# Sample outer products over 128 rows, with the keys held twice, in a hybrid recurrent decoder step

## The chip, the cores and the metric

The kernel runs on one core of one Trainium2 chip. The metric is the device time of one execution in microseconds (us). TensorE (PE) multiplies matrices and writes to PSUM; loading its weights is listed apart as PEld. VectorE (DVE), ScalarE (ACT) and GpSimd (POOL) work element by element, and SyncE (SP) only issues transfers. Each engine works through its own queue in order. Transfers are issued here from the queues of SP and POOL, a few from ACT's.

## The reference, cut to what matters

One inference step of one decoder layer, for a prompt of 256 tokens and for 8 sample sequences of 4 tokens each. Everything is float32. The three branches (an RG-LRU, a gated linear attention or GLA, and an mLSTM) read one projection, their outputs are merged with gates, and a squared-ReLU MLP follows. GLA and mLSTM carry a matrix state for every head and sequence, four heads each:

```python
# GLA, per chunk: state S (128 x 256 per head)
o = einsum('bhid,bhde->bhie', qe, S) + einsum('bhij,bhje->bhie', A, v_)
S = exp(bL[..., 0, :])[..., None] * S + einsum('bhjd,bhje->bhde', k_ * exp(bL - b), v_)
# mLSTM, per chunk: state C (256 x 256 per head), normaliser n
num = ci[..., None] * einsum('bhid,bhde->bhie', q_, C) + einsum('bhij,bhje->bhie', S, v_)
C = cs[..., None, None] * C + einsum('bhj,bhjd,bhje->bhde', wj, k_, v_)
n = cs[..., None] * n + einsum('bhj,bhjd->bhd', wj, k_)
```

For a sample sequence a chunk is its 4 tokens, so a new state is the old one, scaled, plus an outer product of keys and values over 4 tokens. All 8 sequences' states are read, used, updated and written back: 8 tiles of 128x1024 for GLA, and 16 tiles of 128x1028 for mLSTM (a column of each state holds the normaliser).

## The kernel before, in words

**The weight stream.** All large products go through `stream`: tiles of 128x1024 weights are loaded by SP, split by ACT (L156, a rounded part `hi`) and DVE (L157, the rest `lo`) and multiplied in three matmuls per block, L171 to L173, each 128x128 by 128x288 into PSUM tiles named mm. Raw, hi and lo have three buffers each. One step of the stream is one weight tile: 24 matmuls.

**The side work.** The branches' own work is written as generators, `gla()` and `mlstm()`, put beside the stream with `beside`. After each step of the stream, `run` advances each of them by one `yield`. What it issues there has high priority, but is put behind the step's last matmul and its hi and lo. A planner, which works from its own costs, then fixes the order on each engine except SP, whose order is the program's. `issue_after(x)` adds that an instruction may not come before x on the same engine. Of later use are `do(s, f, ...)`, which enters f in the list of step s, and `steps`, which issues one list per yield, in the order of entry. In `mlstm`, `when(n)` is the step of sample tile n, 5 + 3n/2 rounded down, so two tiles take three steps. GLA's tile n has step 3 + 2n.

**The samples.** `parts` writes keys and values, rounded to fp32r, in 128 rows: rows 0 to 63 are for one half of the sequences and rows 64 to 127 for the other, with 16 rows for a sequence, which hold high and low parts of its four tokens. The rows are repeated for all four heads along the free dimension: `kp` holds the keys, `vp` the values. `spread` (L668) makes from one head's values four copies `vx[:, b]`, in each of which only the rows of one sequence of each half are kept. A half call of it writes two of the four copies.

**A tile.** `tile_(n)` of either branch

- multiplies the queries with the old state (L870 or L1254; four products 128x32, side by side in the array, each in two instructions), with the tokens' own part added for the first tile of a head (L872, L1257);
- forms four outer products (L876, L1262), each over the 64 rows of one half, `kp[r, h, ...]` by `vxs[h][r, ...]`, 256 columns wide, into two PSUM buffers `pu` from `misc()` (tiles px, two buffers, shared with all other side work);
- lets DVE scale the old state and add the product (L879, L1267), in mLSTM also the normaliser's column (L1269);
- issues the tile's store from POOL (L880, L1270).

**Loads.** `load(n)` (L856, L1239) issues the load of tile n from POOL. Four buffers take turns: two of tag `st` and two inside a slot. A load of tile n has to wait until the store of tile n-4 has landed. In mLSTM, it is entered four steps ahead of its tile. POOL's queue also carries element-wise work, such as the sums of the merge at L961.

**Values.** In both branches `vx2` holds the spread values of two heads in turn. In mLSTM the two halves for head h are entered two and five steps behind the first tile of head h-1.

Of the kernel before, what the change touches and what calls it, by code (L numbers as in the profile page):

```python
# [8 lines left out]
F32 = mybir.dt.float32  # L9
F32R = mybir.dt.float32r  # L10
AF = mybir.ActivationFunctionType
ALU = mybir.AluOpType
AX = mybir.AxisListType

P = 128
# [38 lines left out]
def trunk(ctx, tc, io):  # L54
    nc = tc.nc
    PSUM = bass.MemoryType.PSUM
    V, S, G, T, Q = nc.vector, nc.scalar, nc.gpsimd, nc.tensor, nc.sync
# [19 lines left out]
    def slot(i, dt=F32):  # L77
        return big.tile([P, 8, N], dt, tag=f"s{i}", name=nm(f"s{i}"))

    def flat(t):  # L80
        return t.rearrange("p a n -> p (a n)")

    def misc():
        return px.tile([P, 512], F32, tag="px", name=nm("px"))
# [12 lines left out]
    def C(n):  # L97
        a, w = COFF[n]
        return con[:, a:a + w]
# [327 lines left out]
    for k in range(KT):  # L427
# [5 lines left out]
        r = slice(32 * (k % 4), 32 * (k % 4) + 32)  # L433
        T.matmul(ps[r, :N], ones[:, 0:32], sq, start=k < 4, stop=k >= KT - 4, skip_group_check=True)
    t = t288()
# [4 lines left out]
    for k, n in ((0, 2), (2, 2), (4, 4), (8, 4), (12, 4)):  # L440
        t = (xa, xb)[k // 8][:, k % 8:k % 8 + n, :]
# [35 lines left out]
    for i, p in enumerate((". L L L LV .", "L LL LL LV LLV .", "L L . L LV . L L . LLV . .", "L L . L LV . L L . LLV . .", "L L L L . V . L L . V .")):  # L477
        k0, k1, _ = STAGES[i]
# [156 lines left out]
    def copies(t):  # L635

        src = ident.rearrange("p (h x g t) -> p h g x t", h=4, x=4, g=2)
        for h in range(4):
            for g in range(2):
                a = P * h + 64 * g  # L640
                G.tensor_copy(t[:, a:a + 64].rearrange("p (x r t) -> p x r t", x=4, r=4), src[:, h, g].unsqueeze(2).to_broadcast([P, 4, 4, 4]))
        return t.rearrange("p (h i) -> p h i", h=4)
# [7 lines left out]
    def parts(dst, src, rep, lo):  # L650

        n, w = dst.shape[1:]
        p = misc()[:, 0:n * w].rearrange("p (h e) -> p h e", h=n)
        for h in range(n):
            T.matmul(p[:, h], rep[:, h], src, start=True, stop=True)
        S.copy(dst, p)
        for h in range(0, n, 256 // w):
            r = slice(h, h + 256 // w)
            t = t288()[:, 0:256].rearrange("p (h e) -> p h e", e=w)
            S.activation(t, p[:, r], AF.Copy, scale=lo[:, 0:1])  # L660
            V.scalar_tensor_tensor(dst[:, r], dst[:, r].bitcast(F32), lo[:, 1:2], t, ALU.mult, ALU.add)

    K_LO, V_LO = C("klo"), C("vlo")

    def spread(vx, v, half):

        for b in range(2 * half, 2 * half + 2):
            S.activation(vx[:, b], v.bitcast(F32), AF.Copy, scale=C("seq")[:, b:b + 1])  # L668
# [31 lines left out]
    def gla():  # L700
# [8 lines left out]
        for h in range(4):  # L709
            p = misc()  # L710
# [23 lines left out]
        dec = sc([P, 4, 12], "dec", 1)  # L734
# [13 lines left out]
        for t in range(2):  # L748
            for q in range(2):
                p = misc()  # L750
# [5 lines left out]
        p = misc()  # L756
# [5 lines left out]
        p = misc()  # L762
# [21 lines left out]
        for t in range(2):  # L784
            p = misc()
# [5 lines left out]
            if t == 0:  # L791
                by_sequence(qm, smp(qe))
                asb = sc([P, NS], "asb", 1)
                p = misc()
# [9 lines left out]
        for h in range(5):  # L804
            if h < 4:
                st = sp.tile([P, 1028], F32, tag="st", name=nm("st"), bufs=2)[:, 0:1024].rearrange("p (c e) -> p c e", c=4)
                pu = misc(), misc()
# [9 lines left out]
            if h:  # L817
                i = h - 1
                po = longp()
                for e in range(2):  # L820
                    for t in range(2):
                        c0 = e * 256 + t * P
                        T.matmul(po[:, c0:c0 + P], vt[:, t, i * 256 + e * P:i * 256 + (e + 1) * P], am[:, t, i, :],
                                 start=e == 0 and t == 0, stop=False, skip_group_check=True)
                for c in range(1, 4):
                    for e in range(2):
                        c0 = e * 256 + c * 64
                        T.matmul(po[:, c0:c0 + 64], sts[i][:, c - 1, e * P:(e + 1) * P], qe[:, i, c * 64:c * 64 + 64],
                                 start=False, stop=True, skip_group_check=True)
# [3 lines left out]
        kv = flat(slot(3, F32R))  # L833
        kp = kv[:, 0:512].rearrange("p (h d) -> p h d", h=4)
        vp = kv[:, 512:1536].rearrange("p (h e) -> p h e", h=4)
        rep = copies(bb[:, 0:512])
        yield
        sums = bb[:, 0:N]
        vx2 = flat(slot(4, F32R))[:, 0:2048].rearrange("p (i b e) -> p i b e", i=2, b=4)
# [4 lines left out]
        tiles, vxs, pos = {}, {}, {}  # L844
# [4 lines left out]

        def second():  # L850
            parts(vp[:, 2:4], vs[:, 0:256], rep[:, 2:4], V_LO)

        def load(n):
            i = n % 4
# [7 lines left out]
        def tile_(n):  # L862
            h, q = n // 2, n % 2
            if q == 0:
                pos[h] = longp()
            po = pos[h]
            s4 = tiles[n][:, 0:1024].rearrange("p (b e) -> p b e", b=4)
            for j in range(4):
                b = 4 * q + j
                T.matmul(po[32 * j:32 * j + 32, 0:256], qm[:, h, NS * b:NS * b + NS], s4[:, j, :], start=q == 0, stop=q == 1, skip_group_check=True)  # L870
            if q == 0:
                T.matmul(po[0:32, 0:256], asb[:, h], vs[:, 0:256], start=False, stop=False, skip_group_check=True)  # L872
            pu = [misc().rearrange("p (i e) -> p i e", i=2) for _ in range(2)]
            for j in range(4):
                b, r = 4 * q + j, slice(64 * (j % 2), 64 * (j % 2) + 64)
                T.matmul(pu[j % 2][:, j // 2], kp[r, h, :], vxs[h][r, b // 2, :], start=True, stop=True)  # L876
            for j in range(4):
                b, s = 4 * q + j, s4[:, j, :]
                V.scalar_tensor_tensor(s, s, dec[:, h, 4 + b:5 + b], pu[j % 2][:, j // 2], ALU.mult, ALU.add)  # L879
            G.dma_start(io["o_gla_s"][n], tiles[n][:, 0:1024])  # L880
            if q == 1:
                pos[h] = sc([P, 257], "os", 1)
                S.copy(pos[h][:, 0:256], po[:, 0:256])
# [175 lines left out]
    def mlstm():  # L1059
# [21 lines left out]
        for h in range(2):  # L1081
            r = slice(4 * h, 4 * h + 4)
# [6 lines left out]
        mr, xr, srow, scol, csb, col = (gates_[n] for n in ("mr", "xr", "srow", "scol", "csb", "col"))  # L1089
# [4 lines left out]
        for t in range(2):  # L1094
            for q in range(2):
                p = misc()
                for i in range(4):
                    n = 4 * q + i
# [5 lines left out]
        p = misc()  # L1104
        for h in range(4):
            for e in range(2):
                n = 2 * h + e
# [3 lines left out]
        p = misc()  # L1111
        for h in range(4):
            for e in range(2):
                n = 2 * h + e
# [3 lines left out]
        for t in range(2):  # L1118
            for q in range(2):
                p = misc()  # L1120
                for i in range(4):
                    n = 4 * q + i
                    T.matmul(p[:, i * P:(i + 1) * P], mc[:, n, t * P:(t + 1) * P], bdk[:, n * P:(n + 1) * P], start=True, stop=True)
                for i in range(2):
                    h = 2 * q + i
# [7 lines left out]
        for n in range(8):  # L1133
            p = misc()
# [6 lines left out]
        p = misc()  # L1141
# [3 lines left out]
        p = misc()  # L1145
# [9 lines left out]
        p = misc()  # L1155
        for h in range(4):
            for e in range(2):
                n = 2 * h + e
# [7 lines left out]
        for h in range(4):  # L1166
            p = misc()
# [6 lines left out]
            p = misc()  # L1174
            for e in range(2):
                n = 2 * h + e
                T.matmul(p[:, 0:256], mc[:, n, 0:P], tf[:, n, 0:NP], start=e == 0, stop=e == 1)
            for e in range(2):
                n = 2 * h + e
# [39 lines left out]
        mn = sc([P, 2], "gn5", 1)  # L1219
        V.tensor_scalar(mn, Pm("mn"), 0.5, None, ALU.mult)  # L1220
        sums = row("rr")
        tiles, vxs, pos, sqs = {}, {}, {}, []
        vx2 = flat(slot(2, F32R))[:, 0:2048].rearrange("p (i b e) -> p i b e", i=2, b=4)
        yield

        def part(dst, src, i, los):
# [9 lines left out]
        def load(n):  # L1236
            i = n % 4
            tiles[n] = sp.tile([P, 1028], F32, tag="st", name=nm("st"), bufs=2) if i < 2 else s9[:, 1028 * (i - 2):1028 * (i - 1)]
            G.dma_start(tiles[n], io["mC"][n])  # L1239

        def values(h, half):
            vxs[h] = vx2[:, h % 2]
            spread(vxs[h], vp[:, h], half)

        def tile_(n):
            h, q = n // 4, n % 4
            if q == 0:
                pos[h] = longp()
            po = pos[h]
            s4 = tiles[n].rearrange("p (b d e) -> p b d e", b=2, d=2)  # L1250
            for i in range(2):
                for d in range(2):
                    b, j = 2 * q + i, 2 * i + d
                    T.matmul(po[32 * j:32 * j + 32, 0:257], qm[:, 2 * h + d, NS * b:NS * b + NS], s4[:, i, d, :],  # L1254
                             start=q == 0, stop=q == 3, skip_group_check=True)
            if q == 0:
                T.matmul(po[0:32, 0:257], psb[:, h], vs, start=False, stop=False, skip_group_check=True)  # L1257
            pu = [misc().rearrange("p (d e) -> p d e", d=2) for _ in range(2)]
            for d in range(2):
                for i in range(2):  # L1260
                    r = slice(64 * i, 64 * i + 64)
                    T.matmul(pu[i][:, d], kp[r, h, d * P:(d + 1) * P], vxs[h][r, q, :], start=True, stop=True)  # L1262
            for i in range(2):
                b = 2 * q + i
                for d in range(2):
                    s = s4[:, i, d, 0:256]
                    V.scalar_tensor_tensor(s, s, csb[:, h, b:b + 1], pu[i][:, d], ALU.mult, ALU.add)  # L1267
                s = s4[:, i, :, 256]
                V.scalar_tensor_tensor(s, s, csb[:, h, b:b + 1], pnb[:, h, :, b], ALU.mult, ALU.add)  # L1269
            G.dma_start(io["o_C_s"][n], tiles[n])  # L1270
            if q == 3:
                pos[h] = sc([P, 257], "os", 1)
                S.copy(pos[h], po[:, 0:257])
# [21 lines left out]
        def do(s, f, *a):  # L1295
            at.setdefault(s, []).append(lambda: f(*a))

        def when(n):
            return 5 + n * 3 // 2
# [3 lines left out]
        do(1, part, kp, ks, 1, K_LO)  # L1303
        do(1, part, vp, vs[:, 0:256], 1, V_LO)
        do(2, ends)
        do(2, values, 0, 0)
        do(3, values, 0, 1)
        for n in range(16):
            do(when(n), tile_, n)
            do(when(n) - 4, load, n)  # L1310
        for h in range(1, 4):
            do(when(4 * h - 4) + 2, values, h, 0)
            do(when(4 * h - 4) + 5, values, h, 1)
        for h in range(4):
            e = when(4 * h + 3)
            do(e + 1, gather, h)
# [148 lines left out]
    h = ff1(0)  # L1465
# [144 lines left out]
```

## Time and profile before

| | us |
|---|---|
| median of 3 runs | 1980.32 |
| lowest and highest | 1979.65, 1981.12 |
| profiled execution | 1977.5 |
| its span, first to last instruction | 1975.7 |
| granted TensorE clock, mean | 0.993 of full |

| engine | busy us | share of the span |
|---|---|---|
| PE | 1940.9 | 98% |
| PEld | 1835.9 | 93% |
| DVE | 1045.2 | 53% |
| ACT | 801.1 | 41% |
| POOL | 233.4 | 12% |

GLA's sample tiles run from about 450 to 512 us of the span, those of mLSTM from about 725 to 832. How to read the rows further down: times are us from the start of the span. A row of the timeline has start, length, engine, line, operation, the tile written `<-` the tiles read, rows*columns of the weights, the moving operand, and how many instructions (`x4`) were merged; in brackets stands the engine's idle time before it and what ended it. A matmul is in flight longer than the distance to the next one, since the array is pipelined: cost is read from start to start. A row of the waits has who waited for whom, us in total, times, the longest. A row of the groups has busy us and the mean ns of one, then the idle time before.

### The profile page before, as it was taken

The page shows a single profiled execution, that of the slowest core. Times are in us where ns is not written, and L with a number is a line of the kernel's source. Part 1 is how long each engine was busy: PE and PEld are TensorE (multiplying, and loading weights), DVE is VectorE, ACT ScalarE, POOL GpSimd, SP SyncE. Part 2 cuts the span into 40 slices and gives each one's busy share as a digit, 9 for nine tenths or more (in the row PEclk, how much of TensorE's full clock was granted, in tenths as well). Part 3 has the DMA queues.
Part 4 walks back from the last instruction along what each step waited for, and adds up shares of the span by engine and source line. Part 5 has one row for each costly group of instructions (what it writes and reads, how often), then busy time and mean ns, then how long its engine had stood idle before and what let it go on. Part 6 is the DMA issues. An engine that isn't in the chain of part 4 may idle for free.

```text
span 1975.7 us, 35634 instructions
## 1 busy us (share of the span) xinstructions
PE 1940.9 (98%) x14944; PEld 1835.9 (93%) x14944; DVE 1045.2 (53%) x1580; ACT 801.1 (41%) x1106; POOL 233.4 (12%) x333
## 2 busy tenths in 40 slices
PE   6999999999999999999999999999999999999997
PEld 5899989998999998899999999999999999999997
DVE  5665737535673456554444564444444445454565
ACT  4233474534454343343333354443333334343433
POOL 0000200011042111101013331000000000010101
PEclk8999999999999999999999999999999999999999
DMA  9887757547443358856778645444444444444443
GB/s 379 341 307 287 289 200 271 203 154 282 163 154 126 129 192 267 311 195 273 278 296 344 239 152 186 156 172 164 163 171 160 160 168 173 166 163 164 161 162 121
DMA packets 109568, 416.99 MB, mean 211 GB/s; under 512 B 11568, under 2 KB 11744, under 8 KB 105696
## 3 DMA queue, kind: packets, MB, share of 16 engines
q1 hardware_dynamic: 100368, 382.34, 52.0%
q0 software_dynamic: 8032, 28.99, 4.3%
q10 hardware_dynamic: 1008, 3.39, 0.5%
q8 instruction: 117, 1.92, 0.4%
q14 instruction: 43, 0.35, 0.0%
HBM read 397.86 MB, written 16.81 MB: 210 GB/s over the span
## 4 chain that ended last, share of the span: by engine, by line
PE 94%; DMA 4%; DVE 1%; issue 0%; ACT 0%; SPq 0%; POOL 0%; DVEq 0%; ACTq 0%; POOLq 0%
PE mm L171 28%; PE mm L173 28%; PE mm L172 28%; PE pa L275 4%; DMA raw<-win 2%; DMA o_C_s<-st 1%; PE px L573 0%; DMA o_C_s<-s 0%; PE px L1262 0%; DVE lo L157 0%; PE px L810 0%; DMA st<-mC 0%; PE px L1189 0%; PE px L128 0%; PE pi L1254 0%
## 5 line engine op out<-in xcount | busy, mean ns | idle before, releaser
L157 DVE TENSOR_TENSOR lo<-raw,hi 128x1024 fp32r<-128x1024 f32 x450 | 556.3, 1238 | 556.0 <-ACT hi L156 536.2
L156 ACT ACTIVATE hi<-raw 128x1024 fp32r<-128x1024 f32 x450 | 476.5, 1060 | 842.0 <-PE mm L172 638.5
L171 PE MATMUL mm<-xh,hi 128*128 128x288 f32 x2576 | 763.4, 300 | 6.3 <-ACT xh L420 5.7
L172 PE MATMUL mm<-xl,hi 128*128 128x288 f32 x2576 | 760.2, 297 | 0.3 <-DVE xl L421 0.3
L173 PE MATMUL mm<-xh,lo 128*128 128x288 f32 x2576 | 744.6, 296 | 0.7 <-DVE lo L157 0.6
L171 PEld LDWEIGHTS mm<-xh,hi 128*128 128x128 f32 x2576 | 482.6, 188 | 27.1 <-issue 9.0
L171 PE MATMUL mm<-s,hi 128*128 128x288 f32 x1664 | 491.4, 298 | 0.3 <-ACT s L942 0.2
L172 PEld LDWEIGHTS mm<-xl,hi 128*128 128x128 f32 x2576 | 485.8, 189 | 3.9 <-issue 1.7
L172 PE MATMUL mm<-s,hi 128*128 128x288 f32 x1664 | 488.2, 295 | 0.0
L173 PEld LDWEIGHTS mm<-xh,lo 128*128 128x128 f32 x2576 | 480.8, 189 | 2.8 <-DVE lo L157 1.2
L173 PE MATMUL mm<-s,lo 128*128 128x288 f32 x1664 | 476.8, 295 | 0.4 <-DVE lo L157 0.4
L171 PEld LDWEIGHTS mm<-s,hi 128*128 128x128 f32 x1664 | 311.8, 188 | 6.6 <-issue 3.7
L172 PEld LDWEIGHTS mm<-s,hi 128*128 128x128 f32 x1664 | 312.5, 188 | 0.3
L173 PEld LDWEIGHTS mm<-s,lo 128*128 128x128 f32 x1664 | 308.3, 188 | 1.1 <-DVE lo L157 0.7
L157 DVE TENSOR_TENSOR lo<-s,hi 128x1024 fp32r<-128x1024 f32 x80 | 98.0, 1225 | 113.8 <-ACT hi L156 113.8
L156 ACT ACTIVATE hi<-s 128x1024 fp32r<-128x1024 f32 x80 | 84.9, 1061 | 140.8 <-PE mm L172 140.1
L1439 POOL TENSOR_TENSOR t<-t 128x288 f32<-128x288 f32 x64 | 60.2, 952 | 639.2 <-ACT t L1438 639.2
L472 DVE TENSOR_TENSOR s<-s,mm 128x288 f32<-128x288 f32 x96 | 41.9, 451 | 42.6 <-PE mm L173 41.7
L275 PE MATMUL pa<-s,silc 128*32 128x128 f32 (+2 forms) x720 | 53.1, 411 | 5.5 <-DMA s<-wad 5.5
L1455 DVE TENSOR_TENSOR s<-s,mm 128x288 f32<-128x288 f32 x96 | 40.3, 450 | 33.9 <-PE mm L173 32.6
L961 POOL TENSOR_TENSOR s<-s,t 128x288 f32<-128x288 f32 x32 | 31.7, 1020 | 190.8 <-DVE t L960 190.8
L275 PEld LDWEIGHTS pa<-s,silc 128*32 128x32 f32 x720 | 21.8, 112 | 23.1 <-issue 10.4
(383 smaller groups left out, 1096.3 us busy)
## 6 DMA issues: line engine op xcount, KB each, us to landing
raw<-win SPq DMA_DIRECT2D x192, 512.0 KB, 4.5
raw<-wf SPq DMA_DIRECT2D x176, 512.0 KB, 4.1
s<-wf SPq DMA_DIRECT2D x80, 512.0 KB, 3.2
s<-wada SPq DMA_DIRECT2D x26, 1024.0 KB, 8.7
s<-wad SPq DMA_DIRECT2D x24, 1024.0 KB, 9.1
ag<-wada SPq DMA_DIRECT2D x22, 1024.0 KB, 5.5
raw<-wout SPq DMA_DIRECT2D x32, 512.0 KB, 5.5
st<-wada SPq DMA_DIRECT2D x20, 512.0 KB, 7.3
```

Of the source, the lines that this page charges most:

```text
L156: pace["hi"] = S.activation(hi, raw, AF.Copy)
L157: pace["lo"] = V.tensor_tensor(out=lo, in0=raw, in1=hi.bitcast(F32), op=ALU.subtract)
L171: T.matmul(pss[m][:, :N], hi[:, kk, ms], xh, start=k == k0, stop=False)
L172: T.matmul(pss[m][:, :N], hi[:, kk, ms], xl, start=False, stop=False)
L173: pace["last"] = T.matmul(pss[m][:, :N], lo[:, kk, ms], xh, start=False, stop=k == kt - 1)
L275: pace["prod"] = T.matmul(ps[32 * j:32 * j + 32, h * w // 4:(h + 1) * w // 4], silu_c(k), v[:, j], start=k == 0 and h == 0, stop=k == KT - ...
L472: V.tensor_tensor(out=dst[:, base + m, :], in0=dst[:, base + m, :], in1=p, op=ALU.add)
L961: G.tensor_tensor(out=a, in0=a, in1=t, op=ALU.add)
L1439: G.tensor_tensor(out=r, in0=r, in1=r, op=ALU.mult)
L1455: V.tensor_tensor(out=a, in0=a, in1=p, op=ALU.add)
```

## The change

- A new helper, `by_half`, makes two copies of the keys on ACT, each scaled with a column of the constant `half`, 1 in the rows of one half and 0 in the others: `kps[0]` is kp itself, with the lower 64 rows kept, `kps[1]` the other.
- The outer products now run over all 128 rows, `kps[i]` by all rows of `vxs[h]`; the zeroed rows leave the other half's part out. The two products of one `pu` buffer stand together, followed by the DVE updates that read them, and then the second buffer's.
- In mLSTM the second keys take the place of one of the two heads' values, so one head's values are held at a time. Their spreads are entered one step behind tiles 4h-2 and 4h-1.
- In mLSTM, load n (from 4 on) is entered one step behind tile n-3 and issued after the store of tile n-3. The first four are as before.

```diff
+    def by_half(kp, other):
+
+        for i, t in ((1, other), (0, kp)):
+            S.activation(t, kp.bitcast(F32), AF.Copy, scale=C("half")[:, i:i + 1])
+        return kp, other
...
 (gla)
+        kps = kp, kv[:, 1536:2048].rearrange("p (h d) -> p h d", h=4)
...
         def second():
             parts(vp[:, 2:4], vs[:, 0:256], rep[:, 2:4], V_LO)
+            by_half(*kps)
...
-            pu = [misc().rearrange("p (i e) -> p i e", i=2) for _ in range(2)]
-            for j in range(4):
-                b, r = 4 * q + j, slice(64 * (j % 2), 64 * (j % 2) + 64)
-                T.matmul(pu[j % 2][:, j // 2], kp[r, h, :], vxs[h][r, b // 2, :], start=True, stop=True)
-            for j in range(4):
-                b, s = 4 * q + j, s4[:, j, :]
-                V.scalar_tensor_tensor(s, s, dec[:, h, 4 + b:5 + b], pu[j % 2][:, j // 2], ALU.mult, ALU.add)
+            for i in range(2):
+                pu = misc().rearrange("p (j e) -> p j e", j=2)
+                for j in range(2):
+                    T.matmul(pu[:, j], kps[j][:, h, :], vxs[h][:, 2 * q + i, :], start=True, stop=True)
+                for j in range(2):
+                    b = 4 * q + 2 * i + j
+                    s = s4[:, 2 * i + j, :]
+                    V.scalar_tensor_tensor(s, s, dec[:, h, 4 + b:5 + b], pu[:, j], ALU.mult, ALU.add)
...
 (mlstm)
-        vx2 = flat(slot(2, F32R))[:, 0:2048].rearrange("p (i b e) -> p i b e", i=2, b=4)
+        v2 = flat(slot(2, F32R))
+        vx = v2[:, 0:1024].rearrange("p (b e) -> p b e", b=4)
+        kps = kp, v2[:, 1024:2048].rearrange("p (h d) -> p h d", h=4)
...
-            G.dma_start(tiles[n], io["mC"][n])
+            with tc.issue_after(stores[n - 3].ins) if n >= 4 else nullcontext():
+                G.dma_start(tiles[n], io["mC"][n])
...
-            vxs[h] = vx2[:, h % 2]
-            spread(vxs[h], vp[:, h], half)
+            vxs[h] = vx
+            spread(vx, vp[:, h], half)
...
-            pu = [misc().rearrange("p (d e) -> p d e", d=2) for _ in range(2)]
-            for d in range(2):
-                for i in range(2):
-                    r = slice(64 * i, 64 * i + 64)
-                    T.matmul(pu[i][:, d], kp[r, h, d * P:(d + 1) * P], vxs[h][r, q, :], start=True, stop=True)
             for i in range(2):
                 b = 2 * q + i
+                pu = misc().rearrange("p (d e) -> p d e", d=2)
+                for d in range(2):
+                    T.matmul(pu[:, d], kps[i][:, h, d * P:(d + 1) * P], vxs[h][:, q, :], start=True, stop=True)
                 for d in range(2):
                     s = s4[:, i, d, 0:256]
-                    V.scalar_tensor_tensor(s, s, csb[:, h, b:b + 1], pu[i][:, d], ALU.mult, ALU.add)
+                    V.scalar_tensor_tensor(s, s, csb[:, h, b:b + 1], pu[:, d], ALU.mult, ALU.add)
...
-            G.dma_start(io["o_C_s"][n], tiles[n])
+            stores.append(G.dma_start(io["o_C_s"][n], tiles[n]))
...
+        do(2, by_half, *kps)
         do(2, values, 0, 0)
...
-            do(when(n) - 4, load, n)
+            do(when(n) - 4 if n < 4 else when(n - 3) + 1, load, n)
         for h in range(1, 4):
-            do(when(4 * h - 4) + 2, values, h, 0)
-            do(when(4 * h - 4) + 5, values, h, 1)
+            do(when(4 * h - 2) + 1, values, h, 0)
+            do(when(4 * h - 1) + 1, values, h, 1)
```

More of the change, by code (lines that the diff above doesn't have):

```diff
@@ L1221, in mlstm @@
         sums = row("rr")
-        tiles, vxs, pos, sqs = {}, {}, {}, []
-        vx2 = flat(slot(2, F32R))[:, 0:2048].rearrange("p (i b e) -> p i b e", i=2, b=4)
+        tiles, vxs, pos, sqs, stores = {}, {}, {}, [], []
+        v2 = flat(slot(2, F32R))
+        vx = v2[:, 0:1024].rearrange("p (b e) -> p b e", b=4)
+        kps = kp, v2[:, 1024:2048].rearrange("p (h d) -> p h d", h=4)
         yield
```

## The prediction

> **What bounds the kernel now.** I read the page first: which engine is full, and what the chain of work that ended last is made of.
>
> ```profile
> PE 1940.9 (98%) x14944; PEld 1835.9 (93%) x14944; DVE 1045.2 (53%) x1580; ACT 801.1 (41%) x1106; POOL 233.4 (12%) x333
> PE 94%; DMA 4%; DVE 1%; issue 0%; ACT 0%; SPq 0%; POOL 0%; DVEq 0%; ACTq 0%; POOLq 0%
> ```
>
> TensorE sets the time: a microsecond taken from its queue is a microsecond of the total, and work elsewhere costs nothing until TensorE waits for it. The second view is busy time by stretch, over the two places that the change touches: the sample tiles of GLA, then those of mLSTM.
>
> ```profile
> 450.00:512.00 62.00, 62.00 (x484) 53.85 (x482) 35.42 (x60) 24.04 (x36) 6.78 (x13) 1.00 0.67 243
> 720.00:835.00 115.00, 112.45 (x841) 94.75 (x841) 70.10 (x148) 37.96 (x53) 22.16 (x36) 1.00 0.82 279
> ```
>
> The columns are length, then busy time and count of PE, PEld, DVE, ACT and POOL, granted clock, DMA share, GB/s. GLA's stretch has no idle PE; mLSTM's has 2.55 us, at full clock. But "busy" hides gaps between pipelined matmuls, so the third view is PE's timeline, read by start times: what does a group of side matmuls add between two matmuls of the weight stream? The groups of matmuls by shape give the changed lines; the timeline shows them in place.
>
> ```profile
> L1262 PE MATMUL px<-s,s 64*128 64x256 f32 x64 | 13.0, 329 | 0.0
> L876 PE MATMUL px<-s,s 64*128 64x256 f32 x32 | 5.0, 329 | 0.0
> ...
> 645.25 0.30 PE L173 MATMUL mm<-xh,lo 128*128 128x288 f32 x1
> 645.38 1.03 PE L1189 MATMUL px<-s,s 128*128 128x257 f32 x4
> ...
> 646.38 0.29 PE L172 MATMUL mm<-s,hi 128*128 128x288 f32 x1
> ...
> 726.22 0.50 PE L1262 MATMUL px<-s,s 64*128 64x256 f32 x4
> ...
> 727.03 0.29 PE L173 MATMUL mm<-xh,lo 128*128 128x288 f32 x1
> ...
> 728.63 0.29 PE L173 MATMUL mm<-xh,lo 128*128 128x288 f32 x1
> 728.85 0.64 PE L1254 MATMUL pi<-st,s 128*32 128x257 f32 x8
> ...
> 729.66 0.30 PE L172 MATMUL mm<-xl,hi 128*128 128x288 f32 x1
> ...
> 731.26 0.29 PE L172 MATMUL mm<-xl,hi 128*128 128x288 f32 x1
> 731.48 0.50 PE L1262 MATMUL px<-s,s 64*128 64x256 f32 x2
> 731.91 0.40 PE L173 MATMUL mm<-xh,lo 128*128 128x288 f32 x1
> 732.15 0.29 PE L171 MATMUL mm<-xh,hi 128*128 128x288 f32 x1
> ...
> 737.02 0.29 PE L173 MATMUL mm<-xh,lo 128*128 128x288 f32 x1
> 737.25 0.64 PE L1254 MATMUL pi<-s,s 128*32 128x257 f32 x8
> 737.82 0.50 PE L1262 MATMUL px<-s,s 64*128 64x256 f32 x4
> ...
> 738.48 0.30 PE L172 MATMUL mm<-xl,hi 128*128 128x288 f32 x1
> ...
> 741.41 0.29 PE L173 MATMUL mm<-xh,lo 128*128 128x288 f32 x1
> ...
> 742.20 0.50 PE L1262 MATMUL px<-s,s 64*128 64x256 f32 x2
> ...
> 742.87 0.29 PE L172 MATMUL mm<-xl,hi 128*128 128x288 f32 x1
> ...
> 829.77 0.50 PE L1262 MATMUL px<-s,s 64*128 64x256 f32 x2
> ```
>
> The stream steps every 0.133 us (727.03 to 728.63 is twelve steps). From 731.26 to 732.15 lie 0.89 us where two steps would take 0.27: one lone pair of half-row products costs 0.62 us. The tile's read products alone (L1254, 128*32) cost 728.63 to 729.66, 0.77 more than two steps. With four half-row products behind them the added time is 1.19 (737.02 to 738.48), with two it is 1.19 as well (741.41 to 742.87): attached to L1254 a group of either size costs 0.43. In the group of four, products of the upper and the lower half run side by side, so they cost no more than two of one half. A lone group of another data type but full 128*128 shape (645.25 to 646.38, four in 0.86, 0.216 each) is far longer in matmul work, yet it fits 257 columns at a constant rate and leaves no room for a fixed part. So I take the half-row pair's cost to be mostly the change of shape, paid on the way in and out.
>
> Counted through that timeline from the first group (726.22) to the last (829.77), mLSTM's 64 products are 15 lone pairs, 5 attached pairs and 6 attached fours; GLA's 32 are 2 lone pairs, 2 attached pairs and 6 attached fours. **Old price:** 17 x 0.62 + 19 x 0.43 = 10.5 + 8.2 = 18.7 us.
>
> **The products over 128 rows.** The same 96 matmuls, each now 128*128 with the other half's rows zeroed in the keys. No row shows this shape with 256 columns in one pass, so I bound it.
>
> ```profile
> 748.98 0.29 PE L171 MATMUL mm<-xh,hi 128*128 128x288 f32 x1
> 749.11 0.30 PE L1280 MATMUL px<-rd,ones 128*128 128x32 f32 x2
> ...
> 749.47 0.30 PE L173 MATMUL mm<-xh,lo 128*128 128x288 f32 x1
> ```
>
> Two tiny 32-column products add 0.22, so 0.11 each is the lower end; the stream's 288-column step of the same data type, 0.133, is the upper end. I take it by columns from the latter, which is nearest: 256/288 x 0.133 = 0.1185. New price 96 x 0.1185 = 11.4 (10.6 to 12.8), **a gain of 7.3 us (5.9 to 8.1)**. By group: a lone pair falls from 0.62 to 0.24, an attached pair from 0.43 to 0.24, an attached four rises from 0.43 to 0.47, since its halves no longer overlap. L1254 keeps its own 0.77. How the planner splits the groups no longer matters, which makes this term robust against another order.
>
> [...]
>
> **Loads behind the next store.** POOL's timeline holds the mC loads (L1239) and the stores (L1270), in one queue in order; PE's timeline shows who waits.
>
> ```profile
> 757.74 0.53 POOL L1239 DMA_DIRECT2D s<-mC  x1 [7.34 <-DMA o_C_s<-s]
> 758.27 0.54 POOL L1270 DMA_DIRECT2D o_C_s<-st  x1
> 766.73 0.53 POOL L1239 DMA_DIRECT2D st<-mC  x1 [7.92 <-DMA o_C_s<-st]
> ...
> 776.25 0.53 POOL L1239 DMA_DIRECT2D st<-mC  x1 [8.45 <-PE px L1280]
> ...
> 783.40 0.64 PE L1254 MATMUL pi<-st,s 128*32 128x257 f32 x8 [0.97 <-DMA st<-mC]
> ...
> 793.43 0.64 PE L1254 MATMUL pi<-s,s 128*32 128x257 f32 x8 [1.57 <-DMA s<-mC]
> ```
>
> Each load waits for the store that frees its buffer, and that store was issued directly behind the load before (757.74, 758.27, then 766.73). So one store's whole flight, some 8 us, lies between successive loads: 9.0 and 9.5 us apart here. The tiles come every 6.5 us (tile 2's L1254 at 737.25, tile 9's due 0.97 ahead of 783.40), so the loads fall behind until PE stands still for 0.97 and 1.57 us. With the change, load n goes behind store n-3 and waits for store n-4, issued a tile earlier: two stores share a flight, so the queue can turn every 4 to 5 us, faster than the tiles. Behind the waiting load on POOL are the next store and the merge's additions (L961); they wait less than now. By step number the load is placed where it was or one step later, and three tiles (19 us) ahead of its use: its own flight of 7.1 us (776.25 to 783.40) fits. **Gain 2.5 us**; bounds 0 (the wait moves to another tile) to 2.55. GLA's loads are not touched, and its stretch has no idle PE.
>
> **Added copies (by_half) and values for one head.** On ACT: two copies of 128x512 and two of 128x1024. The rows for them are the stream's second half (L157), ACT's wait in mLSTM's stretch, a cast at GLA's start and one spread.
>
> ```profile
> L157 DVE TENSOR_TENSOR lo<-raw,hi 128x1024 fp32r<-128x1024 f32 x450 | 556.3, 1238 | 556.0 <-ACT hi L156 536.2
> ...
> ACT hi L156 <- PE mm L172: 62.6, 23, 5.1
> ...
> 448.33 1.08 ACT L156 ACTIVATE hi<-raw 128x1024 fp32r<-128x1024 f32 x1
> ...
> 734.99 0.89 ACT L668 ACTIVATE s<-s,con 128x256 fp32r<-128x256 f32 x2
> ```
>
> The cast of 128x1024 takes 1.08 us (448.33), so I reckon half of it for 128x512: 2 x 0.54 + 2 x 1.08 = 3.2 us at the most. ACT's waiting for PE to free the stream's buffers covers them. In mLSTM's stretch 23 casts waited 2.7 us each on the mean (62.6 / 23). The thin place is GLA's start, where the cast at 448.33 came without a wait, behind side work: 1.1 us more there may show. I take 0, bounds 0 to 3.2. In-place scaling of mLSTM's keys waits for the products that form the normalisers, issued in the same step; two steps remain before the first tile.
>
> The spreads (0.89 per half) are as many as before, but with one buffer they can't run until the last head's tiles have read it. The half for b 0 and 1 moves to the step of tile 4h-1, two steps ahead of tile 4h. Between tile 3 and tile 4 that is about one and a half tile periods, 10 us, against 0.89 and the queue. Cost 0. DVE's updates stay 96; each pair of products is followed by its own pair of updates, so DVE may begin two matmuls earlier, worth nothing off the path. SP's queue is not touched.
>
> **Sum.** 7.3 + 2.5 = 9.8 us. The profiled execution took 1977.5 (span 1975.7 and 1.8 around it), which would become 1967.7; it lies 2.8 under the median of 1980.3, so on the median's scale **1970.5 us**, 0.5% less.
>
> **Rivals.**
> *The waiting load stays, somewhere else.* Only the products gain: 1980.3 - 7.3 = 1973.0. For it: DMA is busy 0.82 of mLSTM's stretch, and stores of 7 to 8 us leave no surplus. Against: loads move ahead by whole tiles.
> *The fixed cost belongs to any lone visit, not to the half-row shape.* Then 0.62 and 0.43 stay and the twelve fours lose their overlap, 12 x 2 x 0.1185 = 2.8 more; less 2.5 for the loads: 1980.6, no change. For it: PE's rows name no cause. Against: the lone L1189 and L1280 groups show no such part (the latter adds 0.22 in all, less than the 0.38 in question).
> *The overlap of the halves is what counts.* If all 96 ran side by side in twos, as in the fours (737.82), and a change of shape cost nothing, 48 slots of 0.1185 would become 96: 5.7 more, less 2.5, 1983.5, still within what counts as no change. Against: they take 18.7 us now, not 5.7, and 24 of 36 groups have one half only. [...]
> *ACT is held by the single values buffer (slower).* If the spread for the next head waits on ACT for the last tile's second pair, the casts queue behind it and PE runs out of weights. Three stream buffers leave two tiles of 24 x 0.133 = 3.2 us, less the cast (1.08) and VectorE's difference behind it (L157, 1.24): about 4.1 us of cover. A hold of X costs X - 4.1, six times (three heads, two halves). It decides above 5.7 us a hold, where the 9.8 are eaten; at 7 us, the time is 1970.5 + 6 x 2.9 = 1988. For it: waits of up to 5.1 us stand on that queue already. Against: the tiles that are read lie a full step back.
>
> **How the numbers follow.** The forecast has 0.60, a larger gain (0.11 or less per product and earlier ends) 0.03, the load wait staying 0.17, the fixed cost staying 0.10, the overlap counting 0.02, ACT held 0.08. A measurement of this kernel tells 0.2%, 4 us, from no change: below 1976.3 is faster, 0.80; within it 0.12; above 1984.3 slower, 0.08. The range: from 1966 (gain of 8.1 + 2.55, and the profile's 2.8 us of scatter) to 1978 (forecast with all 3.2 us of copies uncovered and neither the loads' gain nor the middle of the product bound: 1980.3 - 5.9 + 3.2 = 1977.6).
>
> **What would show it.** Right: lone groups of the new products add about 0.24 a pair, with no wide step around them; PE idle in the mLSTM stretch falls under 0.5; POOL's order is store, load with waits under 3 us. Wrong: pairs still at 0.6; idle PE before L1254 or before the products, released by ACT's L668 or by lo; casts that stop waiting for PE around a head's end.

## The result, and the profile after

The changed kernel took 1966.81 us (median of 4 runs, 1966.03 to 1968.11) against 1980.72 (1979.65 to 1982.64): ratio 0.9932, 95% interval 0.9920 to 0.9944. It was compared twice more below, with 0.9947 (0.9935 to 0.9959) and 0.9933 (0.9921 to 0.9946). By these ratios it is 10.5 to 13.5 us faster; 9.8 were forecast. The time lies inside the stated range of 1966 to 1978, close to its lower end. The profiled execution took 1968.1 with a span of 1966.3, only 9.4 under the profiled one of before. That gap between 9.4 and 13.9 is what the experiments start from.

The page and the two stretches (GLA's sample tiles, mLSTM's), columns as before:

```profile
PE 1934.1 (98%) x14944; PEld 1836.1 (93%) x14944; DVE 1044.2 (53%) x1580; ACT 805.4 (41%) x1110; POOL 235.2 (12%) x333
PE 95%; DMA 2%; DVE 1%; ACT 0%; issue 0%; SPq 0%; DVEq 0%; ACTq 0%
...
450.00:512.00 62.00, 62.00 (x490) 55.52 (x490) 36.33 (x62) 24.29 (x36) 6.79 (x13) 1.00 0.70 245
720.00:835.00 115.00, 115.00 (x917) 102.52 (x916) 74.26 (x156) 41.98 (x58) 22.80 (x36) 1.00 0.87 292
```

The same 14944 matmuls; mLSTM's stretch has no idle PE left (it had 2.55), and 917 matmuls start in the same 115 us instead of 841. PE's timeline shows the new products (L1274) in place; L1266 is the query product that was L1254:

```profile
730.69 0.29 PE L172 MATMUL mm<-xl,hi 128*128 128x288 f32 x1
730.82 0.40 PE L1274 MATMUL px<-s,s 128*128 128x256 f32 x2
731.06 0.29 PE L173 MATMUL mm<-xh,lo 128*128 128x288 f32 x1
...
735.69 0.29 PE L173 MATMUL mm<-xh,lo 128*128 128x288 f32 x1
735.92 0.64 PE L1266 MATMUL pi<-s,s 128*32 128x257 f32 x8
736.49 0.50 PE L1274 MATMUL px<-s,s 128*128 128x256 f32 x2
736.83 0.40 PE L1274 MATMUL px<-s 128*128 128x256 f32 x2
737.06 0.30 PE L171 MATMUL mm<-xh,hi 128*128 128x288 f32 x1
737.20 0.30 PE L172 MATMUL mm<-xl,hi 128*128 128x288 f32 x1
```

A lone pair adds 0.24 us (730.82 to 731.06), and no wide step follows it. The attached four adds 735.69 to 737.20 less two steps, 1.24; without L1266's 0.77 that is 0.47. Per product 0.117 to 0.118 either way. POOL's queue now reads store, load, store, load:

```profile
752.84 0.53 POOL L1280 DMA_DIRECT2D o_C_s<-st  x1 [4.67 <-DVE st L1277]
753.37 0.53 POOL L1251 DMA_DIRECT2D s<-mC  x1
757.69 0.53 POOL L1280 DMA_DIRECT2D o_C_s<-st  x1 [3.79 <-DVE st L1277]
758.84 0.53 POOL L1251 DMA_DIRECT2D st<-mC  x1 [0.62 <-PE mm L172]
765.56 0.53 POOL L1280 DMA_DIRECT2D o_C_s<-s  x1 [6.18 <-DVE s L1279]
766.09 0.53 POOL L1251 DMA_DIRECT2D st<-mC  x1
```

POOL now idles ahead of the stores, waiting for DVE's update, as it should when the loads are not what is late. The load of tile 9 is issued at 766.09; it was 776.25. Further on, two loads waited 3.7 and 4.7 us for a store, more than the 3 that were forecast, and PE did not notice.

### The profile page after: what moved, and what is told of

It is laid out like the page before. It is cut to its first block, busy times and chain, and to the rows that moved or that the text cites. A ratio compares the mean times of both kernels' runs of the same rounds, so it can differ in the third digit from the quotient of the medians.

```text
span 1966.3 us, 35640 instructions
## 1 busy us (share of the span) xinstructions
PE 1934.1 (98%) x14944; PEld 1836.1 (93%) x14944; DVE 1044.2 (53%) x1580; ACT 805.4 (41%) x1110; POOL 235.2 (12%) x333
## 4 chain that ended last, share of the span: by engine, by line
PE 95%; DMA 2%; DVE 1%; ACT 0%; issue 0%; SPq 0%; DVEq 0%; ACTq 0%
PE mm L171 29%; PE mm L173 28%; PE mm L172 28%; PE pa L275 4%; DMA raw<-win 2%; PE px L1274 0%; PE pi L1266 0%; PE px L573 0%; PE px L816 0%; DVE lo L157 0%; PE px L1198 0%; PE px L128 0%; PE px L655 0%; DMA s<-x 0%; PE px L884 0%
## 5 line engine op out<-in xcount | busy, mean ns | idle before, releaser
L275 PE MATMUL pa<-s,silc 128*32 128x128 f32 (+2 forms) x720 | 53.9, 415 | 5.2 <-DMA s<-wad 5.2
L275 PEld LDWEIGHTS pa<-s,silc 128*32 128x32 f32 x720 | 22.1, 114 | 23.1 <-issue 10.3
```

The source lines that it names most:

```text
L275: pace["prod"] = T.matmul(ps[32 * j:32 * j + 32, h * w // 4:(h + 1) * w // 4], silu_c(k), v[:, j], start=k == 0 and h == 0, stop=k == KT - ...
```

## Experiments

**E1: the kernel before once more; E2: its loads alone changed; E3: its products alone changed; E4: the changed kernel again.** One chip. E1 and E4 have no edit. E2 is the kernel before with

```diff
-            G.dma_start(tiles[n], io["mC"][n])
+            with tc.issue_after(stores[n - 3].ins) if n >= 4 else nullcontext():
+                G.dma_start(tiles[n], io["mC"][n])
...
-            do(when(n) - 4, load, n)
+            do(when(n) - 4 if n < 4 else when(n - 3) + 1, load, n)
```

and E3 is the changed kernel with these lines undone.

> The kernel before, unchanged, run once more beside itself, for the scatter and for a second profile. Ratio 1.000 within 0.002. The question is the 4 us by which the timed difference (13.9 us between medians) exceeds that of the two profiled executions (9.4 us). Theory A (the PE wait for mC loads varies from one execution to the next, and the profiled one had a small one): the profile here shows an idle PE of more than the 2.55 us seen before in the stretch of mLSTM's tiles, some 4 to 8 us. Theory B (the profiles differ by something outside the change, such as the start): idle PE there stays at 2 to 3 us, and span differences sit in the first 100 us or in the clock.

> The kernel before with only the mC loads put behind the next store; the products over 64 rows and the values of two heads stay. Theory A (load waits cost more in the mean than in the one profile): 5 to 7 us faster, ratio 0.9965 to 0.9975. Theory B (the profile's 2.5 us is the whole of it): 2.5 us faster, ratio 0.9987. Rival (the wait moves): no change. In all of them PE has no idle time before L1254 for mC if the order store, load holds, and the products' groups cost what they cost before, 0.62 a lone pair.

> The changed kernel with the mC loads entered and ordered as in the kernel before; products over 128 rows and one head's values stay. Theory A: 7 to 8 us faster than before, ratio 0.996, PE idle before L1266 for mC of 2.5 us or more remains in the profile. Theory B: 7.3 us plus nothing, the same ratio, but then loads only and products only add up to 10 us and the rest of the 13.9 us is scatter. A gain near 11 us would mean that the products' term was too small instead.

> The changed kernel, unchanged, on the same chip as the others. Ratio 0.9932 (0.992 to 0.9944) as first measured if the 13.9 us hold; 0.995 if the profiles' 9.4 us are the true difference. Theory A: the sum of the gains of loads only and products only, within 1.5 us.

| | median us | lowest to highest | ratio to before (95%) |
|---|---|---|---|
| before, same chip | 1979.96 | 1976.35 to 1983.41 | |
| E1 | 1980.20 | 1978.05 to 1983.40 | 1.0006 (0.9997 to 1.0015) |
| E2 loads | 1978.04 | 1976.81 to 1978.77 | 0.9993 (0.9984 to 1.0001) |
| E3 products | 1974.66 | 1971.72 to 1977.80 | 0.9978 (0.9970 to 0.9987) |
| E4 both | 1968.08 | 1967.25 to 1968.89 | 0.9947 (0.9935 to 0.9959) |

The parts don't add up: by the ratios 1.4 and 4.4 us alone, 10.5 together (1.9, 5.3 and 11.9 by the medians). Theory A has the direction right, but each of its numbers missed; E1's idle PE is 3.05 us, below its 4 to 8. E4's ratio lies nearer to the 0.995 that was expected for a true difference of 9.4 us; E9, the same kernel further down, gives 0.9933 again. Why the comparisons differ by some 3 us stays open. The timelines give the same without the scatter of whole runs, if time is counted from one matmul of the weight stream to another. From the last one ahead of mLSTM's first tile to the one 800 further on:

| | us |
|---|---|
| before, first profile | 147.08 |
| E1 | 149.10 |
| E2 loads | 146.87 |
| E3 products | 144.36 |
| E4, and the changed kernel's first profile | 137.85 |

Against E1 that is 2.2 and 4.7 alone and 11.2 together. Over the 1000 matmuls around GLA's tiles, before, E1 and E2 take 185.28, E3, E4 and the changed kernel 184.35. So the interaction lies in mLSTM's stretch, and the traces say why. First the load wait, in E1 and then in E3. POOL's row issues the load that PE's timeline then waits for:

```profile
775.49 0.54 POOL L1239 DMA_DIRECT2D st<-mC  x1 [8.26 <-PE px L1280]
...
781.16 0.29 PE L173 MATMUL mm<-xh,lo 128*128 128x288 f32 x1
784.50 0.72 PE L1254 MATMUL pi<-st,s 128*32 128x257 f32 x8 [3.05 <-DMA st<-mC]
785.15 0.61 PE L171 MATMUL mm<-xh,hi 128*128 128x288 f32 x1
785.55 0.44 PE L172 MATMUL mm<-xl,hi 128*128 128x288 f32 x1
785.79 0.44 PE L173 MATMUL mm<-xh,lo 128*128 128x288 f32 x1
```

```profile
772.76 0.53 POOL L1250 DMA_DIRECT2D st<-mC  x1 [7.24 <-DMA o_C_s<-st]
...
777.67 0.29 PE L173 MATMUL mm<-xh,lo 128*128 128x288 f32 x1
781.58 1.08 PE L1265 MATMUL pi<-st,s 128*32 128x257 f32 x8 [3.61 <-DMA st<-mC]
```

The same kernel as before stood 3.05 us here in one go, not 0.97 and 1.57. Its load was issued 0.8 us earlier than in the first profile (775.49 for 776.25), but was 9.0 us in flight instead of 7.1. Behind the stall the stream steps every 0.24 us instead of 0.133. The stretches after it (E1, then E3; the clock is the third number from the end) give the reason:

```profile
780.00:785.00 5.00, 1.95 (x19) 1.37 (x18) 2.02 (x5) 1.06 (x1) 0.00 (x0) 0.99 0.91 310
785.00:790.00 5.00, 5.00 (x26) 4.43 (x22) 2.20 (x5) 0.00 (x0) 2.17 (x4) 0.67 1.02 315
```

```profile
780.00:785.00 5.00, 3.42 (x18) 2.62 (x19) 1.49 (x3) 0.00 (x0) 0.75 (x2) 0.59 1.02 330
785.00:790.00 5.00, 5.00 (x31) 5.00 (x31) 1.95 (x5) 1.46 (x2) 3.90 (x6) 0.73 0.96 351
```

The mean granted clock of the 5 us behind E1's wait is 0.67, which costs an estimated 0.33 x 5 = 1.7 us more, so the wait cost 4.7 by this estimate. The table agrees: E1 is 2.0 longer than the first profile, whose waits were 2.55. In E3 the clock is 0.59 and 0.73; by the same estimate that costs 0.41 x 3.42 + 0.27 x 5 = 2.8, on 3.6 of idle, 6.4 in all. E3's PE gets there 3.5 us earlier (777.67 against 781.16), but its load comes only 2.9 earlier (781.58 against 784.50). It was issued 2.7 earlier, when a store had landed, and was 8.8 us in flight: the chain of stores sets it, and 1.7 of the products' gain is given back there, more of it by the clock than by the wait. From E3 to E4, which differ in the loads alone, the table falls by 6.5 and the medians by 6.6.

The steps follow the clock: where 0.133 us is usual, they take 0.24 in E1 from 785.55 to at least 787.00, and in E3 from 782.99 to at least 785.87. In E1 the mean clock is still 0.99 from 780 to 785, although PE started again at 784.50; in E3, whose wait ended at 781.58, it is 0.59 in that stretch. The waits of 0.97 and 1.57 in the first profile left the clock at 1.00 (780 to 795).

The spread of the runs points the same way without a profile: 5.4 and 6.1 us with the old load order (E1, E3), 2.0 with the new one (E2), eleven runs each. The wait differs from one execution to the next, and the profile of before had caught a shorter one than E1's (2.55 us of idle PE against 3.05).

E2 then should have gained those 4.7 us, and gained 1.4 (-0.2 to 3.2). Its mLSTM stretch has no idle PE, as expected, but the planner, given the loads in another order, has put half-row products inside a group of the conditioning product (L275, 128*32), which stands in one piece before. PE's timeline of E2:

```profile
814.60 0.29 PE L173 MATMUL mm<-xh,lo 128*128 128x288 f32 x1
814.83 1.07 PE L275 MATMUL pa<-ag,silc 128*32 128x512 f32 x8
815.71 1.02 PE L275 MATMUL pa<-s,silc 128*32 128x512 f32 x2
816.66 0.38 PE L1263 MATMUL px<-s,s 64*128 64x256 f32 x1
816.97 1.05 PE L275 MATMUL pa<-s,silc 128*32 128x512 f32 x2
817.95 0.38 PE L1263 MATMUL px<-s,s 64*128 64x256 f32 x1
818.26 1.05 PE L275 MATMUL pa<-s,silc 128*32 128x512 f32 x4
819.24 0.40 PE L173 MATMUL mm<-xh,lo 128*128 128x288 f32 x1
819.48 0.29 PE L171 MATMUL mm<-xh,hi 128*128 128x288 f32 x1
819.70 0.50 PE L1263 MATMUL px<-s,s 64*128 64x256 f32 x2
820.13 0.40 PE L172 MATMUL mm<-xl,hi 128*128 128x288 f32 x1
820.37 0.29 PE L173 MATMUL mm<-xh,lo 128*128 128x288 f32 x1
```

Each entry of one kind among the other is another change of shape: from 814.60 to 820.37 the side work adds 5.24 us to four steps of the stream, where sixteen L275 (2.05) and two lone pairs (1.24) would add 3.29. Over the 800 matmuls E2 takes 146.87 and the kernel before 147.08, of which 2.55 is its wait: 2.3 us came back, 2.0 of them in this group. In the changed kernel the sixteen L275 stand in one piece; what full-row products would cost inside such a group isn't shown.

That closes the sum. Against E1, E2 saves the wait's 4.6 or 4.7 and gives 2.3 back; E3 saves 6.7 by the products (147.08 - 2.55 - 137.85) and gives 1.7 back at the late load; both together save 6.7 and 4.6, the 11.2 of the table.

**E5 to E7: the price of the shape by itself.** One pair of extra products for each of the 128 weight tiles of the first MLP product, results read by nobody; in E5 over rows 0 to 63, in E6 over all rows, in E7 one over each half into two PSUM buffers. E5:

```diff
+                if probe and m == 1:
+                    w0, a0 = hi[:, 0, 0:P], act(0)[0]
+                    p = misc()
+                    for e in range(2):
+                        T.matmul(p[:, 256 * e:256 * e + 256], w0[0:64], a0[0:64, 0:256], start=True, stop=True)
```

> The changed kernel with 128 extra pairs of products in the first MLP product, one pair per weight tile, alone in the stream of 128*128 matmuls, each over the upper 64 rows and 256 columns; their results are read by nobody. Theory (the price of a lone pair of half rows is a change of shape): 0.62 us a pair in the timeline, 128 x 0.62 = 79 us more than the changed kernel, about 2047 us. Rival (the fixed part belongs to any lone visit of another matmul, or to the neighbours in the sample tiles): the same as the kernel with all 128 rows.

> The same 128 extra pairs over all 128 rows. Theory: 0.234 us a pair, 30 us more than the changed kernel, about 1998 us. Rival (fixed part of any lone visit): 0.6 a pair, 79 us more, as with 64 rows.

> The same 128 pairs, one product over the upper and one over the lower 64 rows, into two PSUM buffers. Theory: the two halves run side by side, but the change of shape stays: 0.62 less one product of 0.12 to 0.14, about 0.49 a pair, 63 us more, about 2031 us. Rival (overlap is what counts, the change of shape is cheap): less than the 30 us of the full-row pairs.

They took 2041.9, 1996.8 and 2034.9 us in one run each, 75, 30 and 68 more than the changed kernel's 1967.0 on the same chip (E9). A pair in the timelines of E5, E6 and E7:

```profile
1312.94 0.29 PE L173 MATMUL mm<-xh,lo 128*128 128x288 f32 x1
1313.16 0.50 PE L181 MATMUL px<-xh,hi 64*128 64x256 f32 x2
...
1313.83 0.29 PE L172 MATMUL mm<-xl,hi 128*128 128x288 f32 x1
```

```profile
1305.19 0.29 PE L173 MATMUL mm<-xh,lo 128*128 128x288 f32 x1
1305.33 0.40 PE L181 MATMUL px<-xh,hi 128*128 128x256 f32 x2
...
1305.70 0.29 PE L172 MATMUL mm<-xl,hi 128*128 128x288 f32 x1
```

```profile
1304.83 0.29 PE L173 MATMUL mm<-s,lo 128*128 128x288 f32 x1
1305.06 0.38 PE L181 MATMUL px<-xh,hi 64*128 64x256 f32 x2
...
1305.60 0.30 PE L172 MATMUL mm<-xl,hi 128*128 128x288 f32 x1
```

Less two steps of 0.133, a pair adds 0.62, 0.24 and 0.50. Same weight tile, same place, same columns: the half-row shape is what costs 0.38 more, and running the halves side by side saves 0.12. In eight places of E7 one of the two products stands alone, and it adds 0.50 as well: the second half adds nothing, the change of shape is what is paid. In E5 the 0.38 is spread over four steps, each some 0.1 us longer than in the plain stream: into the pair, between its products, out of it, and the one behind. What in the change takes that time isn't shown. Both rivals fall. E5 came out some 4 us under its expectation; 2 of them are six places with two pairs in one group, at 0.87 instead of twice 0.62, which share one change of shape. E7's 5 us over are for half pairs of 0.51 in the mean where 0.49 was expected. Single runs don't settle the rest.

**E8: fewer changes of the other shape; E9: the changed kernel beside it.** The query products of two neighbouring tiles are entered together (16 instructions of 128*32), in both branches, and the updates behind them. In mLSTM:

```diff
-            do(when(n), tile_, n)
+            do(when(n | 1), reads, n)
+        for n in range(16):
+            do(when(n) + 1, update, n)
```

> The changed kernel with the tile's work in two: the products of queries and old state of two neighbouring tiles (128*32, the other shape in the sample work) are entered together, then the updates of the one and, a step later, of the other. Theory (a change of shape costs about 0.34 us for the way in and out): twelve of twenty-four visits go, 12 x 0.34 = 4 us less than the changed kernel, ratio 0.998 against it; a group of sixteen adds 1.20 us where two of eight added 1.53. Rival (the first tile's update and store come a step later, loads fall behind, PE waits): no gain, idle PE before the products of queries and state.

> The changed kernel, unchanged, beside the one with paired products on the same chip: ratio 0.993 to 0.995 against the kernel before, 4 us more than the paired one by the theory, the same by its rival.

E8 took 1964.87 us (1964.32 to 1965.61, ratio 0.9921, interval 0.9907 to 0.9935), E9 1967.00 (1966.77 to 1968.28, ratio 0.9933). The two sets of five runs don't overlap: 2.1 us faster, half of the 4 expected. Where a pair stayed whole the price was as reckoned:

```profile
737.22 0.29 PE L173 MATMUL mm<-xh,lo 128*128 128x288 f32 x1
737.44 1.07 PE L1272 MATMUL pi<-s,s 128*32 128x257 f32 x16
738.45 0.50 PE L1287 MATMUL px<-s,s 128*128 128x256 f32 x2
738.79 0.40 PE L1287 MATMUL px<-s 128*128 128x256 f32 x2
739.02 0.30 PE L171 MATMUL mm<-xh,hi 128*128 128x288 f32 x1
```

From 737.44 to the products are 1.01 us for two tiles, 0.57 for one (735.92 to 736.49 above). But the planner left only 8 of 12 pairs whole, all four of GLA and four of mLSTM's eight, and split the rest, one of them across a group of the conditioning product: 8 x 0.34 = 2.7. Counted by the stream as above, E8 is 1.9 shorter than E9 in mLSTM's stretch and 0.8 in GLA's, the same 2.7. PE did not wait for loads, so that rival falls too. E8 is the fastest version here.

## Why the prediction was right, point by point

- *The products.* Forecast 18.7 to 11.4 us; after, lone pairs at 0.24 and attached fours at 0.47 give 96 x 0.1175 = 11.3, a gain of 7.4 for 7.3. Counted by the stream it is 6.7 in mLSTM's stretch and 0.9 in GLA's. The constant rate of the lone full-shape group (L1189, 0.216 us a product), which carried the argument, held: E5 and E6 show the fixed part in the half-row shape alone.
- *"How the planner splits the groups no longer matters."* Right where the products stand in the stream or behind query products, and worth more than it was priced at: in E2, half-row products cost 2.3 us in another order. Inside a group of another shape it was not tried.
- *The loads.* The mechanism was right, two stores share a flight: that of 779.58 was issued while the one of 774.01 was in flight, for which the load of 783.82 still waited 3.7 us. The size was not: 2.5 us, with 2.55 as the upper bound, is the wait of one execution. E1 had 3.05 of idle and an estimated 1.7 of low clock. The step that failed is the bound from a single profile, with the load's flight of 7.1 us taken as fixed (9.0 in E1) and no term for the clock; its own hint, that this execution lay 2.8 us under the median, was treated as a constant offset. E1's execution lay 1.8 under its median too, so what the wait costs in the median is not measured.
- *Copies and values at nothing.* Right: GLA's stretch gains 0.93, which is what its products alone should give (2 x 0.62 + 8 x 0.43 less 32 x 0.1175 = 0.92). ACT's queue did come to wait for the last tile's products, the beginning of the slower rival, in the waits of the changed kernel's mLSTM stretch:

```profile
ACT hi L156 <- PE mm L172: 42.8, 20, 3.9
...
ACT s L674 <- PE px L1274: 9.3, 8, 2.5
```

The spreads (L674) were held at most 2.5 us, under the estimated 4.1 of cover, and casts still wait for PE, 42.8 us where it was 62.6.

- *The sum.* On the scale of the two profiles 9.8 were forecast and 9.4 came. From E1 to E4 the two stretches shrink by 11.2 and 0.9, 12.2 together, which is the products' 7.4 and the wait's 4.7; the ratios give 10.5 to 13.5.
- *The range.* That 1966.8 lies inside is in part luck. The gains at their bounds, 8.1 and 2.55, reach only to 1969.7; the rest of the way to 1966 was the 2.8 us entered as scatter of the profile, and rounding. It made up for the loads' term, which was too small.

## What to carry to other kernels

Read the price of a small group of matmuls from start to start across it, not from busy time: here a half-row pair in a dense stream of full-shape matmuls paid 0.38 us more than a full one, and a pair over all rows, half of them zeros, cost 0.24 for the 0.62 of one over half the rows. Where a stall hangs on a chain of transfers, one profile gives one draw of it: look at the spread of the runs before bounding its gain, and price the clock behind it (an estimated 1.7 us in E1, 2.8 in E3). Ask whether a faster engine will give its gain back at the next late transfer, as PE gave back 1.7 us in E3; here two changes that met in one stall were worth more together than apart.

## What the runs showed of the hardware that was not expected

Behind an idle PE of 3.05 us (E1) the granted clock was 0.67 in the mean of 5 us, which cost an estimated 1.7 us on top, and behind 3.61 us (E3) it was 0.59 and 0.73, an estimated 2.8; behind 0.97 and 1.57 us (before) it stayed at 1.00. In E1 the clock fell only behind the wait: it was 0.99 from 780 to 785, when PE had started again at 784.50, and 0.67 from 785 to 790. A change of shape in and out cost 0.38 us for a half-row pair (0.62 in E5 against 0.24 in E6), more than three of the 0.117 us products themselves. One half-row product between matmuls of the stream cost as much as two side by side, 0.50 us (E7).
